# Differential attention inside a hybrid decoder layer: the logits as four 128-row products with a stacked q, the first softmax's sum moved into the row normalisation, and the low part of the probabilities last in a step

## The chip, the cores and the metric

The kernel runs on one core of one Trainium2 chip, as one launch. The metric is the time of that launch in device microseconds (us). Three timed runs of the kernel before gave 857.5, 857.45 and 855.52 us (median 857.45); the profiled execution took 855.89 us.

Engines are named as in the profile: PE is the tensor engine's matmul, PEld its weight load, DVE the vector engine, ACT the scalar engine, POOL the GpSimd engine, SP the engine that issues most DMAs.

## What is computed

A decoder layer on 512 tokens of width 1024: an RMS norm, one combined projection, then two branches side by side (differential attention and a gated linear recurrence), merged by sigmoid gates, and a squared-ReLU MLP. The part that the change touches is the attention: 8 heads, each with two components of 64 dimensions, v of 128.

```python
q = rmsnorm(q, q_g); k = rmsnorm(k, k_g)              # over 64 dimensions
logits = einsum('bqhcd,bkhcd->bhcqk', q, k) * scale   # c = 0, 1
logits = where(rel >= 0, logits + bias, -inf)
p = softmax(logits, axis=-1)
attn = p[:, :, 0] - lam * p[:, :, 1]
out = einsum('bhqk,bkhe->bqhe', attn, v)
out = rmsnorm(out, subln_g) * (1.0 - lambda_init)     # per query row and head, over 128
```

All inputs are float32.

## The kernel before

**Precision.** A float32 operand is kept as two parts in the matmul's reduced format: a high part (a rounded copy, made by ACT) and a low part (what the rounding left, made by DVE: source minus high). `split` makes both. A product of two such operands is three matmuls that accumulate in one PSUM bank: high·high, high·low, low·high (`mm3`, lines 137 to 139). The helper that records every DVE, ACT and POOL operation stands at line 67, so these engines' rows, and some of PE's, all show L67.

**Stages.** First a start-up with the norm of x and two gates; then the attention phase, 77 to 290 us of the span, in which the projection of q, k and v runs interleaved with the attention itself; then the recurrence with the second half of the gates and the output projections; then the MLP. Weights come through SP's DMA queue into `wraw`, are cast to `whi` by ACT and reduced to `wlo` by DVE.

**The attention phase.** Heads are projected in four groups of two. `qkv_pair` makes a group: q, then k, then v, four token tiles of 128 each. After the norm over 64 dimensions (sum of squares, a power on POOL, a multiplication), `turn` in `qkv_pair` transposes a head's q or k (four transposes, line 516) into one PSUM bank, and `split` makes a unit `qkT`: `[:, 0, :]` is the high part, `[:, 1, :]` the low part, with component 0 on partitions 0 to 63 and component 1 on partitions 64 to 127.

`attention` runs 32 steps, head by head, and in each head four blocks of 128 queries; block i sees 128·(i+1) keys. `logits(s)` makes both components' logits, at least 256 columns wide (256, 256, 384 and 512 for the four blocks), by three products each, so six matmuls over 64 rows, components 0 and 1 in turn on the two halves of the rows (line 564). In `soft_a` DVE adds the bias and takes the row maximum (one instruction a component), and ACT does the exponential with its row sum. A step later `soft_b` takes the reciprocals of both sums, scales the first exponential by its own, and adds the second one, scaled by minus lambda over its sum. Another step later `turn` transposes the row block (line 598) and splits it into `pt`; `av` multiplies by v after every second block; `post_a` to `post_d` do the norm over 128 (squares, sums over partitions on PE at line 629, the power on POOL, a round trip through `rdram` that spreads it over partitions) and make `aT`.

A step calls these functions in the order of the list `order`, each for the step it is due at, and then lets `fill_in` emit projection work of the next group worth about 3.6 us. When a new group of heads begins, what is left of its projection is emitted first. DVE, ACT and POOL keep the order in which the program emits; on PE and SP the scheduler places each instruction where its operands are due by its own reckoning.

**The bias.** A table of each head is written to DRAM (`trep`) and read back skewed into `toep`, one buffer for each of the 8 heads.

Of the kernel before, what the change touches and what calls it, by code (L numbers as in the profile page):

```python
# [11 lines left out]
F32 = mybir.dt.float32  # L12
F32R = mybir.dt.float32r
# [24 lines left out]
def tile_block(ctx: ExitStack, tc: tile.TileContext, x, w_in, w_rga, w_rgx, w_pa, w_pr, w_o,  # L38
# [257 lines left out]
    def unit(name, dt=F32R):  # L296
        return actp.tile([P, 2, S], dt, tag="unit", name=name)
# [112 lines left out]
    t2 = {n: wk.tile([P, 2], F32, name=n) for n in ("ls", "le")}  # L410
    t8 = [wk.tile([P, KT], F32, name=n) for n in ("ab", "e", "den", "s", "s2", "po", "tmp", "mxl")]
    wk.tile([P, 32], F32, name="apart2")
    toep = [wk.tile([P, S], F32, tag=f"toep{h}", name=f"toep{h}") for h in range(NH)]
    PT = []
    for half in range(2):
        PT.append([wk.tile([P, 2 + 2 * half, 256], F32R, name=f"pt{half}{z}", tag=f"pt{half}{z}") for z in range(2)])
# [8 lines left out]
    def bias_table():  # L425
        parts = ((0, 512), (512, 128))
        ohs = []
        for c0, n in parts:
            o = work("oh")
            nc.sync.dma_start(o[:64, :n], onehot[:, c0:c0 + n])  # L430
            ohs.append(o)
        rb = sm.tile([64, 32], F32, name="rbt", tag="rbt", bufs=1)
        G.memset(rb, 0.0)
        G.memset(rb[32:33, :], MASKED)
        nc.sync.dma_start(rb[0:NBUCKET, 0:NH], rel_bias)
        yield
        for (c0, n), o in zip(parts, ohs):
            ps = psum("at")
            T.matmul(ps[:32, :n], rb, o[:64, :n], start=True, stop=True)
            tb = work("tb")  # L440
            V.tensor_copy(tb[:32, :n], ps[:32, :n])
            nc.sync.dma_start(tdram[:, c0:c0 + n], tb[:NH, :n])
        yield
        for h in range(NH):
            nc.sync.dma_start(trep[h].rearrange("o (r y) -> o r y", r=P),
                              tdram[h:h + 1, :].rearrange("h (o y) -> h o y", o=1).broadcast_to([1, P, TW]))
            yield
            t0 = trep[h][0:1, :]
            nc.sync.dma_start(toep[h], bass.AP(tensor=t0.tensor, offset=t0.offset + 127, ap=[[TW - 1, P], [1, S]]))

    def lam_diff(lt):
        lv = lt[:, :256].rearrange("p (a b c) -> p a b c", a=2, b=2)
# [36 lines left out]
    def qkv_pair(j, qk, v):  # L489
# [59 lines left out]
    def attention(fills, qks, vs, pads):  # L549
# [5 lines left out]
        def logits(s):  # L555
            h, i = place(s)
            qk = qks[h // 2]
            qT, kT = qk[h % 2, 0], qk[h % 2, 1]
            N = max(256, P * (i + 1))
            lg = [psum("at"), psum("at")]  # L560
            for a, (x0, y0) in enumerate(((0, 0), (0, 1), (1, 0))):
                for c in range(2):
                    r = slice(64 * c, 64 * c + 64)
                    T.matmul(lg[c][:, :N], qT[r, x0, i * P:(i + 1) * P], kT[r, y0, :N], start=a == 0, stop=a == 2)  # L564
            st[s] = lg

        def soft_a(s):
            h, i = place(s)
            n = P * (i + 1)
            lg = st[s]  # L570
            mx = sm.tile([P, 2], F32, tag="mx", name="mx")
            pe = [work("pe") for _ in range(2)]
            for c in range(2):
                V.tensor_tensor_reduce(out=pe[c][:, :n], in0=lg[c][:, :n], in1=toep[h][:, 384 - P * i:512], scale=1.0,
                                       scalar=-3e38, op0=ALU.add, op1=ALU.max, accum_out=mx[:, c:c + 1])
            nm = sm.tile([P, 2], F32, tag="nm", name="nm")
            V.tensor_scalar(out=nm, in0=mx, scalar1=-1.0, scalar2=None, op0=ALU.mult)
            sums = sm.tile([P, 2], F32, tag="sums", name="sums")
            for c in range(2):
                A.activation(pe[c][:, :n], pe[c][:, :n], AF.Exp, bias=nm[:, c:c + 1], accum_out=sums[:, c:c + 1])  # L580
            st[s] = pe, sums

        def soft_b(s):
            n = P * (s % NT + 1)
            pe, sums = st[s]
            rc = sm.tile([P, 2], F32, tag="rc", name="rc")
            V.reciprocal(rc, sums)
            r2 = sm.tile([P, 1], F32, tag="r2", name="r2")
            V.tensor_scalar(out=r2, in0=rc[:, 1:2], scalar1=lneg, scalar2=None, op0=ALU.mult)
            V.tensor_scalar(out=pe[0][:, :n], in0=pe[0][:, :n], scalar1=rc[:, 0:1], scalar2=None, op0=ALU.mult)  # L590
            V.scalar_tensor_tensor(out=pe[0][:, :n], in0=pe[1][:, :n], scalar=r2, in1=pe[0][:, :n], op0=ALU.mult, op1=ALU.add)
            st[s] = pe[0]

        def turn(s):
            i = s % NT
            tp = psum("at")
            for b in range(i + 1):
                T.transpose(out=tp[:, b * P:(b + 1) * P], in_=st[s][:, b * P:(b + 1) * P], identity=ident)  # L598
# [26 lines left out]
        def post_b(h):  # L625
            of, sq = st["of", h]
            ps = psum("at")
            for t in range(NT):
                T.matmul(ps[:, t:t + 1], sq[:, t * P:(t + 1) * P], ones, start=True, stop=True)  # L629
            rs = sm.tile([P, NT], F32, tag="rs4", name="rs4")  # L630
# [17 lines left out]
        def at(step, f, *a):  # L648
            acts.setdefault(step, []).append((f, a))

        for s in range(NH * NT):
            h, i = place(s)
            at(s, logits, s)
            at(s, soft_a, s)
            at(s + 1, soft_b, s)
            at(s + 2, turn, s)
            if i % 2 == 1:
# [683 lines left out]
```

## Time and profile before

| | us |
|---|---|
| median of three timed runs | 857.45 |
| profiled execution | 855.89 |
| its span, first to last instruction | 854.1 |
| mean granted TensorE clock, share of full speed | 0.999 |
| instructions in the span | 13734 |

The span is what the profile's rows are placed in; about 1.8 us of the profiled execution lie around it. A matmul's row has a start and a modelled length, and the lengths of neighbours overlap; how fast PE goes is therefore read from the distance between the starts of consecutive matmuls (the pitch), not from the busy share.

### The profile page before, as it was taken

The page shows a single profiled execution, that of the slowest core. Times are in us where ns is not written, and L with a number is a line of the kernel's source. Part 1 is how long each engine was busy: PE and PEld are TensorE (multiplying, and loading weights), DVE is VectorE, ACT ScalarE, POOL GpSimd, SP SyncE. Part 2 cuts the span into 40 slices and gives each one's busy share as a digit, 9 for nine tenths or more (in the row PEclk, how much of TensorE's full clock was granted, in tenths as well). Part 3 has the DMA queues.
Part 4 walks back from the last instruction along what each step waited for, and adds up shares of the span by engine and source line. Part 5 has one row for each costly group of instructions (what it writes and reads, how often), then busy time and mean ns, then how long its engine had stood idle before and what let it go on. Part 6 is the DMA issues. An engine that isn't in the chain of part 4 may idle for free.

```text
span 854.1 us, 13734 instructions
## 1 busy us (share of the span) xinstructions
PE 847.6 (99%) x5459; PEld 756.2 (89%) x5459; DVE 627.9 (74%) x1069; ACT 448.8 (53%) x703; POOL 85.3 (10%) x102
## 2 busy tenths in 40 slices
PE   9999999999999999999999999999999999999998
PEld 7899999999988887888888888889998998999898
DVE  6765688788865345878866767698787858776797
ACT  7444355544555334695673355654476357536642
POOL 0030222113111101011101100000000000000000
PEclk9999999999999999999999999999999999999999
DMA  6358222132231346757656671515752575456354
GB/s 201 122 163 239 91 69 87 39 111 63 66 103 43 87 135 196 196 173 209 165 157 196 207 263 50 172 25 149 214 179 54 155 237 148 124 150 197 99 143 129
DMA packets 38737, 119.76 MB, mean 140 GB/s; under 512 B 4609, under 2 KB 9417, under 8 KB 38673
## 3 DMA queue, kind: packets, MB, share of 16 engines
q1 hardware_dynamic: 31152, 92.65, 33.3%
q0 software_dynamic: 7520, 26.23, 13.8%
q8 instruction: 43, 0.70, 0.3%
q14 instruction: 22, 0.17, 0.1%
HBM read 102.05 MB, written 11.05 MB: 132 GB/s over the span
## 4 chain that ended last, share of the span: by engine, by line
PE 88%; DVE 5%; DMA 3%; ACT 2%; issue 1%; SPq 0%; ACTq 0%; DVEq 0%
PE acc L67 37%; PE acc L137 14%; PE acc L138 13%; PE acc L139 13%; DMA wraw<-in_w_in_dram 3%; PE at L564 2%; DVE wlo L67 2%; PE at L139 2%; PE at L137 2%; PE at L138 2%; ACT whi L67 1%; PE at L598 1%; PE at L516 1%; PE at L629 1%; DVE pe L67 1%
## 5 line engine op out<-in xcount | busy, mean ns | idle before, releaser
L67 PE MATMUL acc<-h,whi 128*128 128x512 f32 (+1 forms) x656 | 155.8, 331 | 0.0
L67 DVE TENSOR_TENSOR wlo<-wraw,whi 128x1024 fp32r<-128x1024 f32 (+2 forms) x86 | 96.9, 1149 | 78.1 <-ACT whi L67 78.0
L67 PE MATMUL acc<-us,whi 128*128 128x256 f32 (+1 forms) x900 | 153.2, 276 | 0.0
L67 ACT CAST whi<-raw 128x1024 fp32r<-128x1024 f32 x97 | 99.8, 1049 | 88.7 <-DVE raw L67 38.4
L67 PEld LDWEIGHTS acc<-us,whi 128*128 128x128 f32 x900 | 135.6, 188 | 0.4
L67 DVE TENSOR_TENSOR wlo<-raw,whi 128x1024 fp32r<-128x1024 f32 x97 | 117.6, 1219 | 13.6 <-ACT whi L67 13.4
L67 PE MATMUL acc<-us,wlo 128*128 128x256 f32 x448 | 123.7, 276 | 0.0
L67 PEld LDWEIGHTS acc<-h,whi 128*128 128x128 f32 x656 | 110.5, 188 | 12.3
L137 PE MATMUL acc<-whi,hT 128*128 128x256 f32 x384 | 109.9, 286 | 0.0
L67 PE MATMUL acc<-h,wlo 128*128 128x256 f32 (+1 forms) x328 | 108.6, 331 | 0.0
L67 ACT CAST whi<-wraw 128x1024 fp32r<-128x1024 f32 (+2 forms) x86 | 82.5, 981 | 48.1 <-DMA wraw<-in_w_in_dram 32.0
L138 PE MATMUL acc<-wlo,hT 128*128 128x256 f32 x384 | 107.4, 280 | 0.2 <-DVE wlo L67 0.2
L67 PEld LDWEIGHTS acc<-us,wlo 128*128 128x128 f32 x448 | 84.1, 188 | 0.0
L137 PE MATMUL acc<-hT,whi 128*128 128x512 f32 x208 | 82.2, 395 | 0.0
L139 PE MATMUL acc<-hT,wlo 128*128 128x512 f32 x208 | 81.0, 390 | 0.0
L139 PE MATMUL acc<-whi,hT 128*128 128x256 f32 x288 | 80.5, 279 | 0.0
L137 PEld LDWEIGHTS acc<-whi,hT 128*128 128x128 f32 x384 | 72.4, 189 | 4.3 <-issue 3.0
L138 PEld LDWEIGHTS acc<-wlo,hT 128*128 128x128 f32 x384 | 72.3, 188 | 1.0 <-issue 0.5
L67 ACT ACTIVATE pe<-pe,nm 128x128 f32<-128x128 f32 (+3 forms) x64 | 35.5, 556 | 66.0 <-DVE nm L67 66.0
L67 PEld LDWEIGHTS acc<-h,wlo 128*128 128x128 f32 x328 | 61.6, 188 | 6.3
L138 PE MATMUL acc<-hT,whi 128*128 128x512 f32 x156 | 60.9, 390 | 0.0
L67 POOL TENSOR_TENSOR rs<-ms,mhalf 128x8 f32<-128x8 f32 (+1 forms) x25 | 39.7, 1589 | 205.3 <-DVE ms L67 205.3
(205 smaller groups left out, 1625.3 us busy)
## 6 DMA issues: line engine op xcount, KB each, us to landing
wraw<-in_w_in_dram SPq DMA_DIRECT2D x54, 512.0 KB, 3.6
raw<-in_w_dn_dram SPq DMA_DIRECT2D x32, 512.0 KB, 4.4
raw<-in_w_up_dram SPq DMA_DIRECT2D x29, 512.0 KB, 4.1
sum<-in_w_up_dram POOLq DMA_DIRECT2D x18, 512.0 KB, 6.0
raw<-raw POOLq DMA_DIRECT2D x16, 512.0 KB, 4.6
wraw<-in_w_pa_dram SPq DMA_DIRECT2D x8, 512.0 KB, 4.6
wraw<-in_w_pr_dram SPq DMA_DIRECT2D x8, 512.0 KB, 4.6
wraw<-in_w_o_dram SPq DMA_DIRECT2D x8, 512.0 KB, 4.5
```

The lines of the kernel that those rows point to most:

```text
L67: ins = f(*a, **k)
L137: T.matmul(o, l[0], r[0], start=first, stop=False)
L138: T.matmul(o, l[0], r[1], start=False, stop=False)
L139: T.matmul(o, l[1], r[0], start=False, stop=last)
L516: T.transpose(out=ps[:, t * P:(t + 1) * P], in_=qn[t // 2][:, c0:c0 + P], identity=ident)
L564: T.matmul(lg[c][:, :N], qT[r, x0, i * P:(i + 1) * P], kT[r, y0, :N], start=a == 0, stop=a == 2)
L598: T.transpose(out=tp[:, b * P:(b + 1) * P], in_=st[s][:, b * P:(b + 1) * P], identity=ident)
L629: T.matmul(ps[:, t:t + 1], sq[:, t * P:(t + 1) * P], ones, start=True, stop=True)
```

## The change

The change has these parts.

- **q stacked, k doubled.** The unit of q holds, in `[:, c, :]`, the high part of component c on its own 64 partitions and its low part on the other 64. The unit of k holds the high part of component c on both halves. A new tile `kl` (three buffers, zeroed once on POOL) holds the low part of k on the component's own half and zeros on the other. So two matmuls over 128 rows make a component's logits: stacked q with doubled k (high·high plus low·high), and stacked q with `kl` (high·low plus low·0); four a step in place of six over 64 rows.
- **How these units are made.** Each of the 16 units takes two ACT copies and two DVE instructions over 64 partitions in place of one each over 128. The second copy of k's high part is a DMA from SBUF to SBUF on POOL's queue, two for each of 7 heads; the first head's is two more ACT copies.
- **The first softmax's sum.** `soft_b` no longer scales the first exponential by its reciprocal sum: the row is left multiplied by that sum s0, the second exponential is scaled by -lambda·s0/s1, and because the row is normalised over 128 afterwards, it is enough that `post_b` adds EPS·s0² where EPS stood. The sums of a head are kept in one tile.
- **The low part of the probabilities** (`turn_low`) is called last in a step, after `soft_a` and `soft_b`, where it stood directly behind the high part.
- **The bias buffers.** `toep` has three buffers in place of eight; heads 3 to 7 are read during the steps.

```diff
-    toep = [wk.tile([P, S], F32, tag=f"toep{h}", name=f"toep{h}") for h in range(NH)]
+    halves = slice(0, 64), slice(64, P)
+    toep = {}
+    def toep_in(h):
+        toep[h] = wk.tile([P, S], F32, tag="toep", name="toep", bufs=3)
...
+    kl = [wk.tile([P, 2, S], F32R, tag=f"kl{n}", name=f"kl{n}") for n in range(3)]
+    for k in kl:
+        for c in range(2):
+            G.memset(k[halves[1 - c], c, :].bitcast(F32), 0.0)
...
-            d = unit("qkT")
-            split(d[:, 0, :], d[:, 1, :], ps, gsc)
-            qk[hh, qi] = d
+            d = qk[hh, qi] = unit("qkT")
+            def low(dst, c):
+                V.scalar_tensor_tensor(out=dst, in0=ps[halves[c], :], scalar=gsc[halves[c], :], in1=d[halves[c], c, :].bitcast(F32), op0=ALU.mult, op1=ALU.subtract)
+            def high(c, rows):
+                A.activation(d[rows, c, :], ps[halves[c], :], AF.Copy, scale=gsc[halves[c], :])
+            for c in range(2):
+                high(c, halves[c])
+            if qi == 0:
+                for c in range(2):
+                    low(d[halves[1 - c], c, :], c)
+            else:
+                kk = qk[hh, 2] = kl[(2 * j + hh) % 3]
+                for c in range(2):
+                    low(kk[halves[c], c, :], c)
+                for c in range(2):
+                    if j == hh == 0:
+                        high(c, halves[1 - c])
+                    else:
+                        G.dma_start(d[halves[1 - c], c, :], d[halves[c], c, :])
...
-            for a, (x0, y0) in enumerate(((0, 0), (0, 1), (1, 0))):
-                for c in range(2):
-                    r = slice(64 * c, 64 * c + 64)
-                    T.matmul(lg[c][:, :N], qT[r, x0, i * P:(i + 1) * P], kT[r, y0, :N], start=a == 0, stop=a == 2)
+            for c in range(2):
+                for z in (1, 2):
+                    T.matmul(lg[c][:, :N], qT[:, c, i * P:(i + 1) * P], qk[h % 2, z][:, c, :N], start=z == 1, stop=z == 2)
...
-            rc = sm.tile([P, 2], F32, tag="rc", name="rc")
-            V.reciprocal(rc, sums)
+            rc = sm.tile([P, 1], F32, tag="rc", name="rc")
+            V.reciprocal(rc, sums[:, 1, i:i + 1])
             r2 = sm.tile([P, 1], F32, tag="r2", name="r2")
-            V.tensor_scalar(out=r2, in0=rc[:, 1:2], scalar1=lneg, scalar2=None, op0=ALU.mult)
-            V.tensor_scalar(out=pe[0][:, :n], in0=pe[0][:, :n], scalar1=rc[:, 0:1], scalar2=None, op0=ALU.mult)
+            V.scalar_tensor_tensor(out=r2, in0=sums[:, 0, i:i + 1], scalar=lneg, in1=rc, op0=ALU.mult, op1=ALU.mult)
...
-            split(pt[0][:, :i + 1, qs], pt[1][:, :i + 1, qs], tv)
+            hi, lo = (pt[z][:, :i + 1, qs] for z in range(2))
+            A.copy(hi, tv)
+            st["low", s] = lo, tv, hi
+        def turn_low(s):
+            lo, tv, hi = st["low", s]
+            V.tensor_tensor(out=lo, in0=tv, in1=hi.bitcast(F32), op=ALU.subtract)
...
-            rstd_of(rs, ps[:, :NT], P, NT)
+            V.scalar_tensor_tensor(out=se, in0=s0, scalar=EPS, in1=s0, op0=ALU.mult, op1=ALU.mult)
+            V.scalar_tensor_tensor(out=ms, in0=ps[:, :NT], scalar=1.0 / P, in1=se, op0=ALU.mult, op1=ALU.add)
+            G.tensor_tensor(out=rs, in0=ms, in1=mhalf[:, :NT], op=ALU.pow)
...
-        order = [post_d, post_c, post_b, av, post_a, turn, logits, soft_a, soft_b]
+        for h in range(3, NH):
+            at(NT * (h - 3) + 6, toep_in, h)
+        order = [toep_in, post_d, post_c, post_b, av, post_a, turn, logits, soft_a, soft_b, turn_low]
```

What this does to the order of instructions is shown at three places. Rows of the changed kernel carry its own line numbers: its logits are line 593, its transposes of the probabilities line 629. The first place is PE in the last block of head 4 (512 keys). `at` is a PSUM bank of the attention, `pe` the exponentials, `qkT` the units of q and k, `hT` the normed x. Before:

```order
L598 MATMUL at<-ident,pe 128x128 x2
L564 MATMUL at<-qkT 128x512 x6
L137 MATMUL acc<-whi,hT 128x256
L138 MATMUL acc<-wlo,hT 128x256
L139 MATMUL acc<-whi,hT 128x256
```

And now:

```order
L629 MATMUL at<-ident,pe 128x128 x2
L593 MATMUL at<-qkT 128x512
L593 MATMUL at<-kl_487,qkT 128x512
L593 MATMUL at<-qkT 128x512
L593 MATMUL at<-kl_487,qkT 128x512
L139 MATMUL acc<-whi,hT 128x256
L137 MATMUL acc<-whi,hT 128x256
```

Six matmuls over 64 rows became four over 128 rows; the transposes ahead of them and the projection behind them stayed.

The second place is POOL where the third group of heads (4 and 5) begins. `rs` is a power of a norm, `rdram` and `rb` the round trip through DRAM of the norm over 128. Before:

```order
L67 TENSOR_TENSOR rs_2235<-ms,mhalf 128x4
L67 DMA rdram<-rs_2235 128x4
L67 DMA rb<-rdram 128x512
L67 TENSOR_TENSOR rs_2443<-ms,mhalf 128x8
L67 TENSOR_TENSOR rs_2582<-ms,mhalf 128x8
```

And now:

```order
L67 TENSOR_TENSOR rs_2221<-ms,mhalf 128x4
L67 DMA rdram<-rs_2221 128x4
L67 DMA qkT<-qkT 64x512 x4
L67 DMA rb<-rdram 128x512
L67 TENSOR_TENSOR rs_2428<-ms,mhalf 128x8
```

The four DMAs that double k's high part for heads 4 and 5 stand between the two halves of the round trip. On PE, between the last logits of the group before and the first logits that read this doubled k, there stand 73 products of 256 columns and 11 transposes; at the start of the second group it is 78 and 11, and of the fourth 26 of 256 columns, 25 of 512 and 11.

The third place is DVE in the step ahead of that, the last block of head 3. `toep` is the bias, `mx` the maximum, `nm` its negative, `pt` the transposed probabilities (the lower of the two numbers is the high part). Before:

```order
L67 TENSOR_TENSOR pt_495<-at,pt_494 128x2x128
L67 ISA pe,mx<-at,toep_489 128x512
L67 ISA mx 128x1
L67 ISA pe,mx<-at,toep_489 128x512
L67 ISA mx 128x1
L67 TENSOR_SCALAR nm<-mx 128x2
L67 RECIPROCAL rc<-sums 128x2
L67 TENSOR_SCALAR r_2265<-rc,lneg 128x1
L67 TENSOR_SCALAR pe<-pe,rc 128x384
L67 SCALAR_TENSOR_TENSOR pe<-pe,r_2265 128x384
```

And now:

```order
L67 ISA pe,mx<-at,toep 128x512
L67 ISA mx 128x1
L67 ISA pe,mx<-at,toep 128x512
L67 ISA mx 128x1
L67 TENSOR_SCALAR nm<-mx 128x2
L67 RECIPROCAL rc<-sums 128x1
L67 SCALAR_TENSOR_TENSOR r_2245<-sums,lneg,rc 128x1
L67 SCALAR_TENSOR_TENSOR pe<-pe,r_2245 128x384
L67 TENSOR_TENSOR pt_496<-at,pt_495 128x2x128
```

The low part moved from the front of the step to its end, behind the maximum of the new logits and the combination of the two exponentials, and the scaling of the first exponential is gone. The scheduler answers on PE: with a few exceptions, more products of the projection now stand between the transposes of a block and the first product of `av` that reads its low part.

More of the change, by code (lines that the diff above doesn't have):

```diff
@@ L412, in tile_block @@
     wk.tile([P, 32], F32, name="apart2")
-    toep = [wk.tile([P, S], F32, tag=f"toep{h}", name=f"toep{h}") for h in range(NH)]
+    halves = slice(0, 64), slice(64, P)
+    toep = {}
+    def toep_in(h):
+        toep[h] = wk.tile([P, S], F32, tag="toep", name="toep", bufs=3)
+        t0 = trep[h][0:1, :]
+        nc.sync.dma_start(toep[h], bass.AP(tensor=t0.tensor, offset=t0.offset + 127, ap=[[TW - 1, P], [1, S]]))
+    kl = [wk.tile([P, 2, S], F32R, tag=f"kl{n}", name=f"kl{n}") for n in range(3)]
+    for k in kl:
+        for c in range(2):
+            G.memset(k[halves[1 - c], c, :].bitcast(F32), 0.0)
     PT = []
@@ L447, in bias_table @@
             yield
-            t0 = trep[h][0:1, :]
-            nc.sync.dma_start(toep[h], bass.AP(tensor=t0.tensor, offset=t0.offset + 127, ap=[[TW - 1, P], [1, S]]))
+            if h < 3:
+                toep_in(h)
     def lam_diff(lt):
@@ L557, in logits @@
             qk = qks[h // 2]
-            qT, kT = qk[h % 2, 0], qk[h % 2, 1]
+            qT = qk[h % 2, 0]
             N = max(256, P * (i + 1))
             lg = [psum("at"), psum("at")]
-            for a, (x0, y0) in enumerate(((0, 0), (0, 1), (1, 0))):
-                for c in range(2):
-                    r = slice(64 * c, 64 * c + 64)
-                    T.matmul(lg[c][:, :N], qT[r, x0, i * P:(i + 1) * P], kT[r, y0, :N], start=a == 0, stop=a == 2)
+            for c in range(2):
+                for z in (1, 2):
+                    T.matmul(lg[c][:, :N], qT[:, c, i * P:(i + 1) * P], qk[h % 2, z][:, c, :N], start=z == 1, stop=z == 2)
             st[s] = lg
@@ L577, in soft_a @@
             V.tensor_scalar(out=nm, in0=mx, scalar1=-1.0, scalar2=None, op0=ALU.mult)
-            sums = sm.tile([P, 2], F32, tag="sums", name="sums")
+            if i == 0:
+                st["sums", h] = sm.tile([P, 2, NT], F32, tag="sums", name="sums", bufs=3)
+            sums = st["sums", h]
             for c in range(2):
-                A.activation(pe[c][:, :n], pe[c][:, :n], AF.Exp, bias=nm[:, c:c + 1], accum_out=sums[:, c:c + 1])
-            st[s] = pe, sums
+                A.activation(pe[c][:, :n], pe[c][:, :n], AF.Exp, bias=nm[:, c:c + 1], accum_out=sums[:, c, i:i + 1])
+            st[s] = pe
         def soft_b(s):
-            n = P * (s % NT + 1)
-            pe, sums = st[s]
-            rc = sm.tile([P, 2], F32, tag="rc", name="rc")
-            V.reciprocal(rc, sums)
+            h, i = place(s)
+            n = P * (i + 1)
+            pe, sums = st[s], st["sums", h]
+            rc = sm.tile([P, 1], F32, tag="rc", name="rc")
+            V.reciprocal(rc, sums[:, 1, i:i + 1])
             r2 = sm.tile([P, 1], F32, tag="r2", name="r2")
-            V.tensor_scalar(out=r2, in0=rc[:, 1:2], scalar1=lneg, scalar2=None, op0=ALU.mult)
-            V.tensor_scalar(out=pe[0][:, :n], in0=pe[0][:, :n], scalar1=rc[:, 0:1], scalar2=None, op0=ALU.mult)
+            V.scalar_tensor_tensor(out=r2, in0=sums[:, 0, i:i + 1], scalar=lneg, in1=rc, op0=ALU.mult, op1=ALU.mult)
             V.scalar_tensor_tensor(out=pe[0][:, :n], in0=pe[1][:, :n], scalar=r2, in1=pe[0][:, :n], op0=ALU.mult, op1=ALU.add)
@@ L629, in post_b @@
                 T.matmul(ps[:, t:t + 1], sq[:, t * P:(t + 1) * P], ones, start=True, stop=True)
+            s0 = st["sums", h][:, 0, :]
+            se = sm.tile([P, NT], F32, tag="se", name="se")
+            V.scalar_tensor_tensor(out=se, in0=s0, scalar=EPS, in1=s0, op0=ALU.mult, op1=ALU.mult)
+            ms = sm.tile([P, NT], F32, tag="ms", name="ms")
+            V.scalar_tensor_tensor(out=ms, in0=ps[:, :NT], scalar=1.0 / P, in1=se, op0=ALU.mult, op1=ALU.add)
             rs = sm.tile([P, NT], F32, tag="rs4", name="rs4")
-            rstd_of(rs, ps[:, :NT], P, NT)
+            G.tensor_tensor(out=rs, in0=ms, in1=mhalf[:, :NT], op=ALU.pow)
             G.dma_start(rdram[h, :].rearrange("(p t) -> p t", p=P), rs)
@@ L656, in attention @@
             at(s + 2, turn, s)
+            at(s + 2, turn_low, s)
             if i % 2 == 1:
```

## Prediction, made before the changed kernel was run

> **What bounds the kernel now.** I read the page's busy shares and its chain first, then the windows of the attention phase, then what PE waited for there.
>
> ```profile
> PE 847.6 (99%) x5459; PEld 756.2 (89%) x5459; DVE 627.9 (74%) x1069; ACT 448.8 (53%) x703; POOL 85.3 (10%) x102
> PE 88%; DVE 5%; DMA 3%; ACT 2%; issue 1%; SPq 0%; ACTq 0%; DVEq 0%
> 77.00:290.00 213.00, 212.66 (x1591) 190.33 (x1591) 157.73 (x449) 107.63 (x249) 39.85 (x35) 1.00 0.27 81
> 290.00:340.00 50.00, 49.24 (x218) 40.38 (x217) 22.76 (x27) 18.30 (x25) 4.02 (x6) 1.00 0.51 153
> PE at L598 <- DVE po L67: 0.2, 1, 0.2
> PEld at L564 <- issue: 3.2, 19, 0.2
> ```
>
> PE is occupied 99% of the span and holds 88% of the chain. In the attention phase (third row; the columns are length, then busy time of PE, PEld, DVE, ACT and POOL, then granted clock, DMA share and GB/s) it is occupied 212.66 of 213 us at full clock; the only wait for another engine that PE's own rows show there is 0.2 us. DVE is busy 74% and ACT 51% of it. So time in this phase comes off where PE's pitches get shorter, and the last row says where they are long: weight loads at the logits' line idle for a reason that is no other engine.
>
> **The main term: the logits on PE.** The timeline of PE around one step of each width:
>
> ```profile
> 130.78 0.28 PE L138 MATMUL acc<-wlo,hT 128*128 128x256 f32 x1
> ...
> 132.31 0.28 PE L139 MATMUL acc<-whi,tail 128*128 128x256 f32 x1
> 132.42 0.60 PE L598 MATMUL at<-ident,pe 128*128 128x128 f32 x4
> 132.95 0.63 PE L564 MATMUL at<-qkT 64*128 64x256 f32 x6
> 133.51 0.39 PE L137 MATMUL acc<-whi,hT 128*128 128x256 f32 x1
> 133.73 0.28 PE L138 MATMUL acc<-wlo,hT 128*128 128x256 f32 x1
> ```
>
> ```profile
> 211.49 0.27 PE L598 MATMUL at<-ident,pe 128*128 128x128 f32 x1
> 211.69 0.79 PE L564 MATMUL at<-qkT 64*128 64x384 f32 x6
> 212.41 0.39 PE L137 MATMUL acc<-whi,hT 128*128 128x256 f32 x1
> 212.63 0.29 PE L138 MATMUL acc<-wlo,hT 128*128 128x256 f32 x1
> ```
>
> ```profile
> 167.94 0.41 PE L598 MATMUL at<-ident,pe 128*128 128x128 f32 x2
> 168.28 0.96 PE L564 MATMUL at<-qkT 64*128 64x512 f32 x6
> 169.17 0.39 PE L137 MATMUL acc<-whi,hT 128*128 128x256 f32 x1
> 169.40 0.28 PE L138 MATMUL acc<-wlo,hT 128*128 128x256 f32 x1
> ```
>
> ```profile
> 409.65 0.39 PE L138 MATMUL acc<-aT,whi 128*128 128x512 f32 x1
> ...
> 411.47 0.39 PE L137 MATMUL acc<-hT,whi 128*128 128x512 f32 x1
> ```
>
> Full-height pitches first. From 130.78 to 132.31 are 13 matmuls of 256 columns: 0.118 us each. From 409.65 to 411.47 are 8 of 512 columns: 0.2275. For 384, which has no full-height row, I take the middle, 0.173. A transpose takes 0.108: four lie in 0.60 us, of which the last one's length is 0.27.
>
> Now a step of 256 columns. The transposes should end their issue at 132.42 + 4 × 0.108 = 132.85, but the logits start at 132.95: 0.10 us lost on entering. From there to the second matmul behind them is 133.73 − 132.95 = 0.78, of which one ordinary pitch, 0.118, belongs to the projection; the first one behind the logits has 0.22 instead, so 0.10 is lost on leaving too. The six cost 0.10 + 0.78 − 0.12 = 0.76 us. For 384: 0.09 + 0.94 − 0.12 = 0.91. For 512: 0.12 + 1.12 − 0.12 = 1.12.
>
> Six matmuls in 0.56 us between 132.95 and 133.51 are less than six pitches (0.71), so the two row halves do overlap; but they come nowhere near three pitches (0.35), and the borders cost 0.2 more. Four full-height ones, with the same 128 rows as their neighbours and so without these borders, cost 4 × 0.118 = 0.47, 4 × 0.173 = 0.69 and 4 × 0.2275 = 0.91.
>
> Per head there are two steps of 256 and one each of 384 and 512, and 8 heads: 16 × 0.29 + 8 × 0.22 + 8 × 0.21 = **8.1 us less on PE**.
>
> The Trainium skill ("TensorEngine Tiling (Array Packing)", Overview, Theoretical Speedup) says that row tiling of a contraction of 64 or less is worth up to two times. By that the six would have cost three pitches and four full ones would be dearer by one pitch a step, an estimate of 16 × 0.118 + 8 × 0.173 + 8 × 0.2275 = 5.1 us more. The same page (Tiling Modes, Key Properties) also says that changing the tiling mode drains the engine; the 0.10 us before and behind the logits agree with that, and the rows decide for 8.1 us less.
>
> **The other edits, on DVE and ACT.** The groups, and two copies for the question whether fewer partitions are faster:
>
> ```profile
> L67 DVE TENSOR_SCALAR pe<-pe,rc 128x512 f32<-128x512 f32 x8 | 3.8, 478 | 0.0
> L67 DVE TENSOR_SCALAR pe<-pe,rc 128x384 f32<-128x384 f32 x8 | 3.3, 411 | 0.0
> L67 DVE TENSOR_SCALAR pe<-pe,rc 128x256 f32<-128x256 f32 x8 | 2.8, 345 | 0.0
> L67 DVE TENSOR_SCALAR pe<-pe,rc 128x128 f32<-128x128 f32 x8 | 2.2, 277 | 0.0
> L67 DVE SCALAR_TENSOR_TENSOR qkT<-at,qg,qkT 128x512 fp32r<-128x512 f32 x8 | 6.0, 747 | 2.5 <-ACT qkT L67 2.5
> L67 DVE SCALAR_TENSOR_TENSOR qkT<-at,smt,qkT 128x512 fp32r<-128x512 f32 x8 | 6.0, 747 | 4.5 <-ACT qkT L67 4.5
> L67 DVE TENSOR_SCALAR ms<-at 128x4 f32<-128x4 f32 x8 | 1.2, 156 | 3.5 <-PE at L629 3.4
> L67 DVE COPY rb<-acc x1: 692/692/692, 27.6 to 27.6; 128x512 f32<-128x512 f32 x1
> L67 DVE COPY tb<-at x2: 269/474/680, 56.3 to 56.9; 32x512 f32<-32x512 f32 x1, 32x128 f32<-32x128 f32 x1
> L67 ACT ACTIVATE qkT<-at,smt x8: 664/688/695, 74.6 to 227.6; 128x512 fp32r<-128x512 f32 x8
> ```
>
> A copy of 32 partitions by 512 took 0.68 us and one of 128 by 512 took 0.69, so I cost the 64-partition halves at the full duration; the other end, half of it, would only help. DVE loses the scaling of the first exponential, 3.8 + 3.3 + 2.8 + 2.2 = 12.1 us, and gains 16 × 0.75 = 12.0 for the second halves and 8 × 0.16 = 1.3 in `post_b`: 1.2 us more, on 157.7 of what will be some 205 (77%). ACT gains 16 × 0.68 and two more copies for the first head, 12.3 us, on 107.6 (to 58%). Both lie beside a full PE and cost nothing as long as PE's operands come in time. The five bias loads move behind projection weights in SP's queue and are due six steps ahead of the head's first one; the zeroing of `kl` stands on POOL where that of `pt` stands, ahead of the whole phase. Nothing for either.
>
> **The low part last.** DVE waited 19.6 us for ACT's high part in this phase:
>
> ```profile
> DVE pt L67 <- ACT pt L67: 19.6, 18, 6.4
> ACT pe L67 <- DVE nm L67: 66.0, 32, 3.8
> ```
>
> Last in the step, that wait has the maximum and the combination ahead of it, and ACT, which waits 66.0 us for the maximum, gets it earlier. None of this was PE's wait, so no gain is counted. The price: the low part comes later by the maximum and combination of a step, and `av` on PE reads it. In most odd blocks the order now has more products ahead of that read; the tightest with such a delay is the last block of head 6, with 7 products of 512 columns, 5 of 256, 3 of 384 and a transpose: 2.8 us, against about 3.3 that the high part, the maximum, the combination and the low part need in a row (an estimate from their rows). I allow 0.5 us in all; the bounds are 0 and 16 such reads at 0.5, 8 us.
>
> **The doubled k, a new wait.** The first logits of heads 2, 4 and 6 wait for ACT's high part and then a DMA on POOL. PE executes in order, so whatever stands behind these logits waits with them.
>
> ```profile
> 174.43 0.72 ACT L67 ACTIVATE pe<-pe,nm 128x512 f32<-128x512 f32 x1 [3.75 <-DVE nm L67]
> 175.86 0.66 ACT L67 ACTIVATE qkT<-at,smt 128x512 fp32r<-128x512 f32 x1
> rdram<-rs POOLq DMA_DIRECT2D x8, 2.0 KB, 2.2
> rb<-rdram POOLq DMA_DIRECT2D x8, 256.0 KB, 3.7
> ```
>
> The logits ahead ended at 169.17, and ACT reached k's high part at 175.86, behind that step's exponentials: 6.7 us. Then 0.66 for the first half, and 2.2 to 3.7 from issue to landing (POOL's smallest and its 256 KB transfer; this one has 128 KB, nearer the middle, 3.0): 9.6 to 11.1. By the order shown ahead, PE has 78 products and 11 transposes at the second group (10.4 us by the pitches), 73 and 11 at the third (9.8), 26 of 256, 25 of 512 and 11 at the fourth (9.9). The stalls are 0 to 0.7, 0 to 1.3 and 0 to 1.2; I take 0, 0.5 and 0.4, sum 0.9, bounds 0 and 3.2.
>
> **Sum:** −8.1 + 0.5 + 0.9 = −6.7 us. The profiled execution (855.89, span 854.1) would become 849.2, the span 847.4. That execution lies 1.6 below the median of the timed runs; the mean of all four times shown is 856.6, and I forecast 849.9.
>
> **The rivals.**
>
> *The new waits are longer.* If a landing takes 5 us, as a loaded queue could make it, the three group starts stall some 2.2 us each, and the low parts cost 1 more: about 2 us is left, 854. For it speaks that the chain through ACT is long already; against it that the DMA share there is only 0.27. Chance 0.16.
>
> *The gain is given back behind the attention.* Between 290 and 340 us PE was busy 49.24 of 50 us with weights that arrive just in time; if these are paced by their transfers and not by PE, what PE gains ahead is waited for there: 856, no change. Against it: the casts wait for buffers that PE frees, so they move forward with it. Chance 0.08.
>
> *Slower: the chain between ACT and DVE sets the step.* The two wait for each other (66.0 us above), and ACT's 12.3 us and DVE's 1.2 of new work stand inside that chain. It decides from the point at which the transposes wait for `soft_b` more than 0.25 us a step on average (8.1 over 32); then PE's saving isn't felt and the new work is: 855.9 + 13.5 = 869. Against it stands PE's wait of 0.2 us in the whole phase. Chance 0.05.
>
> *Slower: the halves overlap better than I read*, so that four full-height matmuls take a pitch more a step: 855.9 + 5.1 = 861. The timeline's starts speak against it. Chance 0.02.
>
> **How the numbers follow.** The forecast, 847 to 852, has 0.69. The bounds of the waits alone give 848.5 (none) up to 852 (3.2 at the group starts), and the first rival reaches 855. A range of 847 to 855.5 leaves out a little at the bottom, most of the no-change case and the slower ones, under 0.2. Of the first rival's 0.16 about 0.10 is still faster by 0.3% (2.6 us, about what a measurement of this kernel can tell from no change), so faster has 0.79, same 0.06 + 0.08 = 0.14, slower 0.07.
>
> **What would show it.** Right: PE's matmul count is 64 lower (192 to 128 at the logits), the weight loads' idle time there is gone, and the window of the attention phase is about 7 us shorter while those behind it keep their length. The waits would show as PE or PEld waiting at the logits' line for a DMA of `qkT`, and at the products with `pt` for DVE. Wrong: the attention window shorter by under 4 us, DVE or ACT as releasers of PE at the transposes, or a window behind it that grew.

## The result and the profile after

The changed kernel took 863.05 us (median of 4 runs, 862.37 to 866.42), the kernel before, on the same chip, 856.49: a ratio of 1.0088, with an interval of 1.0060 to 1.0115. By this ratio, and by the means of the runs (863.72 and 856.23), it is 7.5 us **slower**, where 6.7 us less had been forecast; the two medians lie 6.6 us apart. A gain or loss that is worked out from ratios below is given in us of the same 856.5. The profiled execution took 862.37 us. One run of the experiments, 1205.85 us at a granted clock of 0.655 (in b96), stands outside its ratio.

The page of the changed kernel begins:

```profile
span 860.6 us, 13700 instructions
PE 852.0 (99%) x5395; PEld 764.7 (89%) x5395; DVE 632.4 (73%) x1061; ACT 462.4 (54%) x721; POOL 95.8 (11%) x122
PE 86%; DVE 6%; ACT 5%; issue 1%; DMA 1%; SPq 0%; DVEq 0%
```

PE has the 64 matmuls less that the change says (5459 to 5395), and yet it is occupied 4.4 us longer: what it still does takes longer. First the place of the edit itself, the timeline of PE around two steps:

```profile
133.90 0.61 PE L629 MATMUL at<-ident,pe 128*128 128x128 f32 x4
134.27 0.36 PE L593 MATMUL at<-qkT 128*128 128x256 f32 x1
134.47 0.28 PE L593 MATMUL at<-kl,qkT 128*128 128x256 f32 x1
134.58 0.28 PE L593 MATMUL at<-qkT 128*128 128x256 f32 x1
134.70 0.28 PE L593 MATMUL at<-kl,qkT 128*128 128x256 f32 x1
134.82 0.28 PE L139 MATMUL acc<-whi,tail 128*128 128x256 f32 x1
134.94 0.28 PE L137 MATMUL acc<-whi,hT 128*128 128x256 f32 x1
...
144.91 0.38 PE L629 MATMUL at<-ident,pe 128*128 128x128 f32 x2
...
146.06 0.28 PE L138 MATMUL acc<-wlo,hT 128*128 128x256 f32 x1
146.18 0.28 PE L139 MATMUL acc<-whi,hT 128*128 128x256 f32 x1
```

From the transposes' start to the second projection matmul behind the logits a step of 256 takes 134.94 − 133.90 = 1.04 us; before it was 133.73 − 132.42 = 1.31. For 512 it takes 146.18 − 144.91 = 1.27 against 169.40 − 167.94 = 1.46. So these two steps became shorter, by 0.27 and 0.19 where 0.29 and 0.21 had been worked out.

What PE waited for from 77 to 290 us (us in total, times, longest):

```profile
PE at L666 <- ACT osq L67: 2.1, 3, 0.9
PE at L629 <- DVE pe L67: 0.3, 1, 0.3
PE at L593 <- ACT qkT L67: 0.2, 1, 0.2
```

These waits of 2.6 us in all are new. PE stands for ACT's squares at the sums over partitions in `post_b`. Where the time goes after that is read from the starts of PE's first and last matmuls of each phase, in us from the start of the span:

| | before | changed | e1, below | h1, below |
|---|---|---|---|---|
| last logits | 270.05 | 269.45 | 269.88 | 261.80 |
| first product with `h` (up projection) | 530.47 | 528.85 | 528.33 | 522.58 |
| last matmul | 849.86 | 856.33 | 847.54 | 842.28 |
| first `h` to last matmul | 319.39 | 327.48 | 319.21 | 319.70 |

Of the 8 us only 1.6 are there when the up projection begins, and then 8.1 us are lost in a phase that the change doesn't touch. The timelines show this loss in the pitch of identical instructions, first before, then changed:

```profile
799.99 0.39 PE L67 MATMUL acc<-h,wlo 128*128 128x512 f32 x1
...
802.03 0.39 PE L67 MATMUL acc<-h,wlo 128*128 128x512 f32 x1
```

```profile
803.66 0.39 PE L67 MATMUL acc<-h,wlo 128*128 128x512 f32 x1
...
806.46 0.39 PE L67 MATMUL acc<-h,wlo 128*128 128x512 f32 x1
```

Every third matmul is one with `wlo`. Before, 9 matmuls lie between the two rows: 2.04 / 9 = 0.2267 us each. Now 12 lie between them: 2.80 / 12 = 0.2333. Nothing waits there; the columns, the engine and the granted clock (1.00 in both) are the same. The windows of 36 us in the products with `us`, before and changed, say it as a count of matmuls, 320 and 310:

```profile
732.80:768.80 36.00, 36.00 (x320) 36.00 (x318) 30.07 (x39) 16.61 (x21) 2.58 (x3) 1.00 0.58 163
```

```profile
736.10:772.10 36.00, 36.00 (x310) 35.98 (x309) 29.68 (x38) 17.02 (x21) 2.58 (x3) 1.00 0.58 161
```

What differs is where the tiles lie. In pool `sm` each small tile takes 32 bytes of a partition. `sums` went from four buffers to three and the new `se` has four: 96 bytes more, and each tile allocated behind `sm` on that side (`hu`, `R`, `h2`, one of two `us` buffers) starts 96 bytes higher. The weight tiles in the pool `wp`, `hT` and `mT`, which are allocated ahead of it, stay. The diff doesn't say that this matters, but the kernel's text does: `weight_pair` begins its tiles 0, 64 or 192 bytes into their buffers according to the product that they serve, and tiles named `apart`, `apart2` and `pad` hold nothing. So the placement of before looks chosen.

### The profile page after: what moved, and what is told of

It reads as the page before. It is cut to its first block, busy times and chain, and to the rows that moved or that the text cites. A ratio compares the mean times of both kernels' runs of the same rounds, so it can differ in the third digit from the quotient of the medians.

```text
span 860.6 us, 13700 instructions
## 1 busy us (share of the span) xinstructions
PE 852.0 (99%) x5395; PEld 764.7 (89%) x5395; DVE 632.4 (73%) x1061; ACT 462.4 (54%) x721; POOL 95.8 (11%) x122
## 4 chain that ended last, share of the span: by engine, by line
PE 86%; DVE 6%; ACT 5%; issue 1%; DMA 1%; SPq 0%; DVEq 0%
PE acc L67 38%; PE acc L138 13%; PE acc L137 13%; PE acc L139 13%; ACT pe L67 2%; DVE pe L67 2%; PE at L139 1%; PE at L137 1%; PE at L138 1%; PE at L593 1%; ACT qkT L67 1%; DVE wlo L67 1%; ACT whi L67 1%; DVE kl L67 1%; DMA wraw<-in_w_in_dram 1%
## 5 line engine op out<-in xcount | busy, mean ns | idle before, releaser
L67 PE MATMUL acc<-h,whi 128*128 128x512 f32 (+1 forms) x656 | 159.1, 336 | 0.0
L67 PE MATMUL acc<-us,whi 128*128 128x256 f32 (+1 forms) x900 | 157.2, 279 | 0.0
L137 PE MATMUL acc<-whi,hT 128*128 128x256 f32 x384 | 108.2, 282 | 0.0
L139 PE MATMUL acc<-whi,hT 128*128 128x256 f32 x288 | 80.1, 278 | 0.0
```

Of the source, the lines that this page charges most:

```text
L67: ins = f(*a, **k)
L137: T.matmul(o, l[0], r[0], start=first, stop=False)
L139: T.matmul(o, l[1], r[0], start=False, stop=last)
```

## The experiments on the placement

**e1_se_one_buffer** gives `se` one buffer; `sm` then has the size that it had before. Changed kernel:

```diff
-            se = sm.tile([P, NT], F32, tag="se", name="se")
+            se = sm.tile([P, NT], F32, tag="se", name="se", bufs=1)
```

> The changed kernel with one buffer instead of four for the small tile se of post_b, so that everything allocated behind the pool sm stands at the addresses of before (in the changed kernel it stands 96 bytes higher). Theory A (placement: matmuls whose moving operand or weights stand 96 bytes off take longer): the pitch of the MLP's 256-column products falls from a mean of 0.117 back to 0.113 us, all the slow groups (us, h, R, hu) give back about 10 us, and the time is 853 us (850.5 to 855). Rival B (the MLP is slower because the changed order meets other transfers or writes there): pitches stay at 0.117, time 862 to 864.

**b96_before_shifted** is the kernel before with 96 unused bytes; b64 and b32 have 64 and 32.

```diff
+    sm.tile([P, 24], F32, name="shifted", bufs=1)
```

> The kernel before with an unused tile of 96 bytes at the end of the pool sm, and nothing else. Theory A: the pitches of us, h, R and hu rise as in the changed kernel, and the time rises by about 10 us, to 866 (863 to 869). Rival B: no change, 856 to 857.

> The kernel before with 64 unused bytes there. Theory A with a period of 64 bytes: no change, 856 to 857, and 32 as bad as 96; with a period of 128 or more: slower by 3 to 15 us. Rival B: no change, 856 to 857.

> The kernel before with 32 unused bytes there. Theory A: slower than before by 0 to 15 us; which groups slow down shows the period of the effect. If only a shift by a multiple of 32 mattered nothing would change, but then 96 would do nothing either. Rival B: no change, 856 to 857.

Measured: e1 853.75 us (11 runs), a ratio of 0.9972 (0.9960 to 0.9983) to before. b96 867.26 (4 runs), 1.0121 (1.0094 to 1.0147). b64 865.26 and b32 869.82 (one run each). The 96 bytes alone cost the old kernel some 10 us, and taking them from the changed kernel gives 1.0088 − 0.9972 = 0.0116 back, 9.9 us. In e1 a window over the products with `us` holds 320 matmuls again:

```profile
730.50:766.50 36.00, 36.00 (x320) 36.00 (x319) 30.13 (x39) 16.82 (x21) 2.58 (x3) 1.00 0.57 162
```

An offset of 64 bytes cost some 9 us and one of 32 some 14, as far as one run each can tell. An offset of 128 was not tried.

Is it the moving tile's own address that counts, or its distance from the weights? **g1_all_shifted** puts the 96 bytes ahead of the weights' pool as well, so that both move.

```diff
+    cp.tile([P, 24], F32, name="shifted")
     hb = cp.tile([P, 16], F32, name="hb")
```

> The kernel before with 96 unused bytes ahead of the weights' and the hidden states' pools instead of behind them: now every tile of the left side stands 96 bytes higher, the weight tiles too, so moving tile and weights keep their distance in nearly all products (only aT, on the right side, stays, some 190 products of 512 columns). Theory A1 (the distance between moving tile and weight tile decides): 227 ns for the h products of 512 columns and 113 for most of us, 1 to 2 us more for aT, 857 to 859. Theory A2 (the moving tile's own address decides): 233 and 116 to 118 as in the changed kernel, 865 to 868.

Measured: 858.85 us (10 runs), 1.0022 (1.0011 to 1.0033). In its timeline 9 matmuls of `h` take 799.23 − 797.19 = 2.04 us again, while in that of b96, shown second, 12 take 2.80 (the step from 809.26 to 810.66 is 6 in 1.40):

```profile
797.19 0.39 PE L67 MATMUL acc<-h,wlo 128*128 128x512 f32 x1
...
799.23 0.39 PE L67 MATMUL acc<-h,wlo 128*128 128x512 f32 x1
```

```profile
809.26 0.39 PE L67 MATMUL acc<-h,wlo 128*128 128x512 f32 x1
...
810.66 0.39 PE L67 MATMUL acc<-h,wlo 128*128 128x512 f32 x1
```

So for these products the **distance** between the moving tile and the weight tile decides. Of the 1.9 us that g1 still loses, 1.1 lie in the products of `aT`, whose tile stayed where it was while its weights moved (0.233 us each where they had 0.227). Put beside the tiles' start addresses in before, changed, e1, b32, b64, b96 and g1, the pitches fall into these groups (distance modulo 128 bytes, median pitch):

| columns | best distance | next | worst |
|---|---|---|---|
| 512 | 0: 227 ns | 64: 229 | 32 or 96: 232 to 234 |
| 256 | 64: 113 to 114 | 0: 118 to 120 | 32 or 96: 116 to 119 |

The groups hold whichever of the two tiles moved: `h` at 64, 32 and 96 bytes (mod 128) has 227 ns as long as its weights stand at the same. The kernel before had almost every product at its best distance.

With 512 columns little else was seen to matter. With 256 the distance is not all: in g1, with the distances of before, a stretch of such products went at a median pitch of 0.118 us where before has 0.113. A window in it holds 232 matmuls; one of the same length over these products of before, shown first, holds 241:

```profile
604.60:631.60 27.00, 27.00 (x241) 27.00 (x239) 20.43 (x20) 16.04 (x19) 0.00 (x0) 1.00 0.73 234
```

```profile
606.20:633.20 27.00, 27.00 (x232) 27.00 (x231) 19.50 (x19) 15.10 (x18) 0.00 (x0) 1.00 0.69 226
```

And in the kernel before the projection beside the attention has 0.118 us at 131 us and (170.89 − 169.51) / 12 = 0.115 at 170 us, with no tile moved in between. What makes these slower was not found.

## The experiments on the logits

With the placement put right the change is faster, but by 2.4 us (0.9972) where the logits save about 8. **Each edit alone.** f1 has the stacked logits without the moved sum and with the low part directly behind the high one; f2 the other way round has only the moved sum and the late low part; f3 is e1 with the low part directly behind the high one. In all three tiles lie as before.

```diff
             A.copy(hi, tv)
             st["low", s] = lo, tv, hi
+            turn_low(s)
-            at(s + 2, turn_low, s)
```

> Only the stacked logits (with their units, DMAs and the three bias buffers); the fold of the first sum and the low part last are undone; addresses behind sm as before. Theory C (the logits on PE give 8 us, and late operands from ACT and DVE take back what the kernel with restored addresses misses): without the fold DVE carries 12 us more, so operands come later than in that kernel: 854 to 856, with more waits of PE. Rival D (the fold and the low part last are what costs, since the low part comes late): 849 to 851.

> The kernel before with only the fold of the first sum and the low part last, same addresses behind sm. Theory C: DVE loses about 11 us of work beside a full PE and nothing on PE changes: 855 to 857, within 0.3% of before. Rival D: 858 to 860, with PE waiting for the low part.

> The kernel with restored addresses (853.75), its low part of the probabilities again directly behind the high part. Theory C: DVE waits again for ACT's high part ahead of the maximum (some 20 us of waits in all) and ACT gets its maximum later, so PE waits more: 854 to 856. Rival D: 851 to 852.5.

Measured: f1 865.81 us, 1.0111 (1.0098 to 1.0124); f2 857.05, 1.0009 (1.0001 to 1.0018); f3 865.95, 1.0114 (1.0093 to 1.0136). The late low part, with the moved sum, gains nothing for the old logits (f2 is 0.8 us slower, if anything), but without it the stacked ones lose 0.0142, 12.2 us. f1 and f3 differ by the moved sum alone, and take the same time: beside the early low part, what the moved sum takes off DVE (12.1 us by the prediction's rows) is worth nothing. Beside the late one it was not tried alone. The direction of f1 and f3 had been expected, not the size. The longest of PE's waits of f3 from 77 to 290 us, and three of its windows (columns as in the prediction):

```profile
PE at L527 <- DVE qn L67: 6.0, 4, 2.7
PE at L667 <- ACT osq L67: 1.8, 3, 0.9
```

```profile
176.00:179.00 3.00, 0.49 (x3) 0.50 (x4) 3.00 (x5) 1.15 (x3) 0.00 (x0) 0.84 0.39 116
179.00:182.00 3.00, 3.00 (x18) 3.00 (x18) 2.78 (x12) 0.82 (x3) 1.61 (x2) 0.59 0.68 238
233.00:236.00 3.00, 3.00 (x11) 2.51 (x11) 2.79 (x12) 0.59 (x1) 1.62 (x2) 0.50 0.80 264
```

DVE comes late with the normalised q and k (`qn`); PE stands up to 2.7 us for them (busy 0.49 of 3 us in the first window), and in the stretches behind such waits the granted clock was 0.59 and 0.50. What DVE waits for ahead of the maximum, and what the attention phase looks like as a whole, stands here, f3 first and e1 second:

```profile
DVE pt L67 <- ACT pt L67: 12.3, 10, 3.4
77.00:290.00 213.00, 203.60 (x1485) 189.66 (x1485) 156.41 (x434) 115.50 (x259) 45.66 (x47) 0.98 0.30 88
```

```profile
DVE pt L67 <- ACT pt L67: 0.4, 1, 0.4
77.00:290.00 213.00, 210.67 (x1540) 197.55 (x1539) 160.86 (x440) 119.99 (x266) 47.79 (x50) 0.99 0.31 94
```

With the low part early, DVE waits 12.3 us for ACT's high part, PE is idle 9.4 us in place of 2.3, and the lower clock, 0.98 against 0.99, is worth some 2 us more of the 213 (an estimate). That is 9 of the 12 us.

**Moving the waits.** e1's own PE waits are 2.0 us for `osq`. Four kernels try to take them away: f4 squares ahead of the copy; g6 and g8 put the sums behind the step's transposes, or last in the step; g5 puts them one step later.

```diff
-        order = [toep_in, post_d, post_c, post_b, av, post_a, turn, logits, soft_a, soft_b, turn_low]
+        order = [toep_in, post_d, post_c, av, post_a, turn, logits, soft_a, soft_b, turn_low, post_b]
```

(g8; g6 has `post_b` between `turn` and `logits`; g5 has `at(s + 5, post_b, h)` and `at(s + 6, post_c, h)`; f4 swaps the two lines of ACT in `post_a`. In the four texts that follow, "the run before" is g5 for g6, and g6 for g8.)

> The kernel with restored addresses (853.75), in which post_a takes the square before the copy, so that the square that the sums over partitions wait for ends a copy (0.58 us) sooner. Theory C (PE's three or four waits for the square, 2.0 to 2.5 us in all, are ACT being late): these waits fall to 0.5 to 1 us, the time to 852 to 852.8. Rival E (PE only waits there for what it would wait for a little later): waits move to other lines and the time stays at 853.5 to 854.

> As the run before, but the sums stay in their step and go behind its transposes: 2.7 to 5.8 us of products ahead of them. Theory C: waits for osq under 0.5 us in sum, 851 to 853. Rival E: 853 to 855.

> As the run before, but the sums last in their step: 2.7 to 6.7 us of products ahead of them. Theory C: no wait for osq, 850 to 852.5. Rival E: 853 to 855.

> The changed kernel with one buffer for se (tiles behind as before) and the sums of the squares, with the read of their result, one step later; the square stands 5 to 10 us of products ahead of the sums instead of 1.1 to 3.8. Theory C (the waits for ACT's square and the half clock behind the longest of them cost 2 to 4 us of e1): PE's waits for osq are 0, no stretch of 3 us at half clock near 170 us, 850 to 852.5. Rival E (the time comes back as another wait for ACT or DVE in the same steps): 853 to 855.

Measured: f4 854.42 us, 0.9975 (0.9961 to 0.9988); g6 854.51, 0.9970 (0.9957 to 0.9983); g8 855.21, 0.9976 (0.9964 to 0.9988); g5 870.47, 1.0143 (1.0090 to 1.0197). None gained on e1. In f4, where 0.5 to 1 us had been expected, the wait for `osq` stayed at 2.0. What PE waits for most in g8, and below it all that it waits for in e1, over the attention:

```profile
PE at L629 <- DVE pe L67: 3.4, 6, 0.9
```

```profile
PE at L666 <- ACT osq L67: 2.0, 3, 0.9
PE at L593 <- ACT qkT L67: 0.3, 1, 0.3
```

How the longest of e1's waits comes about stands in its timelines of DVE, ACT and PE (in brackets idle time before, and what ended it):

```profile
162.26 1.51 DVE L67 SCALAR_TENSOR_TENSOR qkT<-at,qg,qkT 64x512 fp32r<-64x512 f32 x2
163.80 1.10 DVE L67 TENSOR_TENSOR of<-of,rb 128x512 f32<-128x512 f32 x1
```

```profile
164.94 0.73 ACT L67 ACTIVATE aT<-of,sg 128x512 fp32r<-128x512 f32 x1 [2.72 <-DVE of L67]
165.69 0.58 ACT L67 COPY of<-at 128x512 f32<-128x512 f32 x1
166.17 0.60 ACT L67 ACTIVATE osq<-at 128x512 f32<-128x512 f32 x1
```

```profile
166.83 1.05 PE L666 MATMUL at<-ones,osq 128*128 128x1 f32 x8 [0.89 <-ACT osq L67]
```

The two low parts of a turned q hold DVE for 1.51 us; behind them stands the normalisation of the finished head, for which ACT waits at `aT`, and behind that stand the copy and the square of the next head, for which PE waits. So here a doubled instruction on DVE reaches PE through ACT's queue. Once the sums no longer wait, the transposes do, for the combination on DVE. The theory that the place of the sums was at fault fell. In g5 this wait of the transposes grew to 10.7 us.

**h2_transposes_one_step_later** asks whether PE waits for the length of the softmax's way or for the load on it: the transposes, the low part, the products with v and the sums stand one step later.

```diff
-            at(s + 2, turn, s)
-            at(s + 2, turn_low, s)
+            at(s + 3, turn, s)
+            at(s + 3, turn_low, s)
...
```

> The changed kernel with one buffer for se and the transposes of the probabilities, their low part, the products with v and the sums of squares one step later, so that the softmax has a step more before PE reads it. If PE waits for the length of the softmax's way: no wait over 0.5 us, 848 to 851.5. If it waits because DVE and ACT have as much work as PE has time in these steps, or because the five buffers of pe are now all taken: waits as long or longer, 853 to 862.

Measured: 868.65 us, 1.0123 (1.0084 to 1.0162), with PE waiting 9.2 us for ACT at the products with `pt`. More distance doesn't help, so it isn't the length alone. Whether the load on the two engines or the five buffers of `pe`, all taken then, is behind the new waits, this run doesn't tell apart.

**Taking the doubled work away.** In the change, q and k are split by instructions of 64 partitions, two for each one before. h1 has one of 128 again on both engines; h6 doubles only DVE's, h7 only ACT's. The logits of these three are not the reference's, but the matmuls are the same in number, width and order of steps.

```diff
-            for c in range(2):
-                high(c, halves[c])
+            A.activation(d[:, 0, :], ps, AF.Copy, scale=gsc)
...
+                low(kk[:, 0, :])
```

> The changed kernel with one buffer for se, and q and k split as before, by one instruction of 128 partitions for the high part and one for the low part (as many on ACT and DVE as in the kernel before; two DMAs a k as in the change). The two halves of a head are not taken apart, so the logits are not the reference's; matmuls, widths and order of steps stay. Theory H (the doubled split, some 11 us on ACT and 12 on DVE in a phase of 200, is what PE waits for): PE's waits for osq and pe under 0.5 us in sum, no half clock, 847 to 850.5. Rival F (PE, 8 us faster, has caught up with the softmax's own way through DVE and ACT): the waits stay at 1.5 to 3 us, 852.5 to 855.

> h1 with the low parts of q and k on DVE in two instructions of 64 partitions again (12 us more on DVE), the high parts on ACT in one; the halves of a head are not taken apart, the logits are not the reference's. If ACT's doubled copies make PE wait: as h1, 848 to 850. If DVE's do: 852 to 854.5. If each gives half: 850 to 852.

> h1 with the high parts of q and k on ACT in two instructions of 64 partitions again (some 11 us more on ACT), the low parts on DVE in one; the halves of a head are not taken apart, the logits are not the reference's. If ACT's doubled copies make PE wait: 852 to 854.5. If DVE's do: 848 to 850. If each gives half: 850 to 852.

Measured: h1 848.88 us, 0.9901 (0.9873 to 0.9929); h6 852.09, 0.9948 (0.9929 to 0.9967); h7 852.72, 0.9955 (0.9938 to 0.9972). All that PE waited for in the attention of h1:

```profile
PE at L624 <- DVE pe L67: 0.3, 1, 0.3
```

And a window over the logits' phase of e1 and of h1:

```profile
78.00:270.00 192.00, 189.67 (x1427) 179.53 (x1427) 150.25 (x419) 110.51 (x250) 44.65 (x46) 0.99 0.32 95
```

```profile
77.00:262.00 185.00, 184.45 (x1423) 176.52 (x1422) 139.42 (x406) 100.64 (x235) 44.13 (x45) 1.00 0.33 98
```

h1 is through its logits 7 us sooner: DVE is busy 10.8 us less and ACT 9.9 less, PE stands idle 0.55 us in place of 2.33, and the clock stays at 1.00. Not all of the 7 us are delay: between its first and last logits e1 has 132 products of 512 columns and h1 120, and these 12 (some 2.7 us) come later in h1. The last matmuls of the two lie 847.54 − 842.28 = 5.3 us apart. Idle time is 1.8 of that, and a stretch at half clock behind the wait shown above 1.6 (from 167.74 to 172.43 us e1 takes 4.69 us for what the changed kernel, without such a stretch, does in 3.08). The rest was not taken apart. Nor does the half clock set e1's time: six of its eleven runs have a mean clock of 1.000 and took 853.9 us on the mean, the other five 854.0.

By the ratios, 0.9972 and 0.9901, the doubled split costs 6.1 us. Each engine's share alone costs much of it: 0.0047 (4.0 us) with DVE's, 0.0054 (4.6) with ACT's. h6 came out where it had been expected if DVE's copies alone counted, and h7 where it had been expected if ACT's did; so neither alone is the cause. Their intervals overlap, and which of the two is dearer stays open.

**h4_one_copy_for_k** tries to keep some of that with the right logits: k's high part by one ACT instruction, and four DMAs from its tile.

```diff
+    kt = wk.tile([P, S], F32R, name="kt")
...
+                A.activation(kt, ps, AF.Copy, scale=gsc)
...
+                        G.dma_start(d[rows, c, :], kt[halves[c], :])
```

> The changed kernel with one buffer for se, and k's high part (from the second head on) read from PSUM by one ACT instruction of 128 partitions into a tile of its own, from which four DMAs fill the four quarters of the stacked k; this takes 7 of the 16 added ACT instructions away, some 4.8 us, and leaves DVE's 12 us; one toep buffer less makes the room. Theory H: about a third to a half of the 5 us between e1 and h1 comes back, 850.5 to 852.5. Rival: DVE's half of the doubled split sets the wait, 853 to 855. A third outcome: the fourth DMA lands later than the second did and PE waits for it at the first logits of a pair, over 855.

Measured: 859.07 us, 1.0032 (1.0017 to 1.0048). It has a wait of its own; ACT's row from 77 to 290 us:

```profile
ACT kt L67 <- DMA qkT<-kt: 12.9, 3, 4.3
```

The single `kt` must be read by the DMAs of one head before ACT writes the next, up to 4.3 us, and the engines behind follow. That this wait is the whole of its loss is argued from the row alone: h4 also has one `toep` buffer less, and two tiles `kt` were not tried. Of the kernels that compute the reference none came out clearly below e1, 853.75 us.

## Why the prediction was wrong

1. **PE bounds the kernel.** Held: 99% in both.
2. **The main term, −8.1 us.** Right in mechanism and size. With the other two costs taken away, in h1, the time falls by 0.0099, 8.5 us (6.1 to 10.9). h1 has the moved sum and the late low part as well; f2 shows that these gain nothing by themselves.
3. **The sum's missing term, +9.9 us: the step that failed most.** The sum was "−8.1 + 0.5 + 0.9", the terms of instructions and waits alone; what the two small tiles of the moved sum push was put at nothing without being asked, though the kernel's text, with its shifted weight tiles and its empty tiles, hints at placement. Matmuls 260 us and more behind the last logits became up to 3% longer (0.2267 to 0.2333). The prediction named "a window behind it that grew" as a sign of being wrong, and that is what the profile showed, but for none of its rivals' reasons: the second rival had such a window wait for transfers, and PE waited for nothing there.
4. **ACT's 12.3 us and DVE's 1.2, costed at nothing.** "Both lie beside a full PE and cost nothing as long as PE's operands come in time": they did not come in time. The cost was 6.1 us (e1 against h1). The means, DVE 77% and ACT 58%, hid it: the doubled instructions come in clumps, where a q or a k is turned, and other work that PE needs stands behind them, as the rows of e1 show for DVE's queue at 162 to 166 us; for ACT's doubled copies only the time of h7 shows it. The DVE term was moreover netted (12.1 off against 13.3 on). What went off lay in every step and brought nothing (f1 against f3), and what came on stands in the clumps. The third rival came near: the new work in the chain between ACT and DVE. But its sign was the transposes waiting for `soft_b`, where e1 waits at the sums over partitions, and its price was wrong: it had the whole saving lost and 13.5 us added, 869, at a chance of 0.05; the doubled split takes about three quarters of the saving.
5. **The low part last, +0.5 us.** Wrong in sign. Beside the old logits it changes nothing (f2), beside the stacked ones it saves 12.2 us (e1 against f3). The row with DVE's 19.6 us of waits for ACT's `pt` stood in the prediction; as PE's wait for it was nothing, no gain was counted. Beside the stacked logits, with point 4's load and with PE some 8 us faster, such waits do reach PE (f3).
6. **The doubled k's DMA, +0.9 us.** Measured nothing: PE has no wait for it in the changed kernel, and the transfer landed in 2.3 us at the median, less than the 3.0 that were taken:

```profile
qkT<-qkT POOLq DMA_DIRECT2D x14, 128.0 KB, 2.3
```

7. **The bias loads and the zeroing, nothing.** No row of PE's waits in the changed kernel names them; they weren't tried alone.

Together: −8.5 from the logits (before to h1), +6.1 from the doubled split (h1 to e1) and +9.9 from the placement (e1 to changed) make +7.5, the measured 0.0088 of 856.5. That it adds up is no proof, since each number is the step from one run of this chain to the next; the proof of each is its own experiment. And that e1, 853.75 us, lies inside the forecast's range is luck: the doubled split was missed, and the late low part, forecast as a small loss, keeps 12 us away.

## What to carry to other kernels

A diff that adds or drops a tile, however small, moves all that is allocated behind it: list which tiles move against which, and when a window far from the edit changes its pitch with no wait in it, restore the old addresses before believing anything else. Work on an engine that is busy 77% on the mean is not free beside a full one: look at the steps in which it comes in a clump, and at what stands behind it there. And before dropping an edit that does nothing by itself, take it out of the whole and measure: here such an edit keeps 12 us of loss away from the other.

## What was not expected of the hardware

The pitch of a matmul depended on the distance of its operands in memory: 0.227 us at 0 and 0.232 to 0.234 at 32 or 96 bytes modulo 128 for 512 columns, 0.113 at 64 and up to 0.120 at 0 for 256. With 256 columns it rose to 0.118 in some stretches at an unchanged distance, too. Why the best distance differs between the two widths was not tried.

A wait of PE of about a microsecond can be followed by a lower granted clock. In e1 PE waited 0.9 us at 167 us, and then:

```profile
169.00:172.00 3.00, 3.00 (x13) 2.80 (x13) 1.96 (x2) 2.70 (x5) 0.00 (x0) 0.50 0.02 5
```

13 matmuls in 3 us at a clock of 0.50. The changed kernel, with the same wait at the same place, had 25 there at full clock, so this doesn't follow every such wait:

```profile
169.00:172.00 3.00, 3.00 (x25) 2.78 (x24) 1.81 (x5) 3.00 (x7) 0.00 (x0) 1.00 0.02 5
```
